# Contrast adjustment on one core: whole 32 KB rows, single first loads, and a first store that waits for the fifth load

## The chip, the cores and the metric

The kernel runs on one core of one Trainium2 chip. The metric is the time of one execution on the device in microseconds, as the median of several runs; lower is better. A profiled execution of the same program gives the trace. Its span runs from the first to the last instruction of the core, so it is a little shorter than the time that is measured around a run.

## The reference

```python
def setup_inputs():
    batch, c, h, w = 16, 3, 512, 512
    return {
        "x": np.random.rand(batch, c, h, w).astype(np.float32),
        "factor": np.float32(1.5),
    }

def reference(x, factor):
    mean = np.mean(x, axis=(2, 3), keepdims=True)
    return np.clip(mean + factor * (x - mean), 0, 1).astype(np.float32)
```

There are 48 images (16 x 3) of 512 x 512 numbers. Each number is moved away from its own image's mean by a factor of 1.5 and clipped to 0..1. The mean of an image must be known before any of its numbers can be written. Input and output are 50.33 MB each.

## The kernel before

**Tiles.** An image is 32 rows of `ROW` = 8192 numbers (32 KB a row). Four images make a tile of 128 rows, one to a partition, 4.19 MB; there are 12 tiles. On chip lies one tensor `ring` with `BUFS` = 6 slots (L64), and tile t lives in slot t modulo 6, is changed in place there and is stored from there. So load t + 6 can start only when store t has landed.

**Work on a tile.** `load` (L66 to L74) issues a DMA from the SP queue; with n = 2 it takes two tiles in one DMA, and either of them can be used only when the whole has landed. `add` (L86 to L90) is one activation on ScalarE (ACT) that copies the tile onto itself and adds up each row into a column of `sums`. `shift_by` (L92 to L96) multiplies the row sums by `blockw`, a block-diagonal matrix that holds (1 - factor) / pixels, on TensorE: each row gets its image's (1 - factor) x mean in `bias`, in PSUM. Each such product shows as two matmul records in the trace. `clip` (L76 to L84) is two instructions on VectorE (DVE): multiply by the factor and add the bias (L78), then cut to 0..1 (L82). `store` (L98 to L99) issues a DMA from the ACT queue.

**Queues and order.** The order is written out by hand (L101 to L126), and each engine takes its instructions in that order. ACT both computes the adds and issues the stores; a store that waits for its clip holds up the adds behind it, and an add that waits for its load holds up the stores behind it. SP only issues loads. Both queues' transfers run on the same 16 DMA engines.

**The start.** Tiles 0 and 1 are loaded by single DMAs, tiles 2 and 3 by one, tiles 4 and 5 by one. Tile 0 is summed in two halves at once, columns 0 to `SUM` = 4352 by a reduction on DVE (L108) and the rest by ACT. Its clip and store go in three pieces that end at `CUTS` = 1024, 3072 and 8192 columns, that is in rows of 4, 8 and 20 KB.

**The loop** over tiles 1 to 11 (L119 to L126) does, for tile t: the product, the clip, the add of tile t + 1, the store of t, and the load of t + 6. All its loads and stores are whole tiles.

Of the kernel before, what the change touches and what calls it, by code (L numbers as in the profile page):

```python
# [1 line left out]

# [4 lines left out]


P = 128  # L10
ROW = 8192
BUFS = 6
CUTS = (0, 1024, 3072, ROW)
SUM = 4352


@with_exitstack
def kernel(
    ctx: ExitStack,
    tc: tile.TileContext,  # L20
    x: bass.AP,
    factor: float,
    out: bass.AP,
):

    nc = tc.nc
    f32 = mybir.dt.float32
    Alu = mybir.AluOpType  # L30
    Act = mybir.ActivationFunctionType

    B, C, H, W = x.shape
    n_img, n_pix = B * C, H * W
    ppi = n_pix // ROW
    per_tile = P // ppi
    n_tiles = n_img // per_tile
    assert ppi * ROW == n_pix and per_tile * n_tiles == n_img

    factor = float(factor)  # L40
    wconst = (1.0 - factor) / float(n_pix)

    x_f = x.rearrange("b c h w -> (b c h w)")
    out_f = out.rearrange("b c h w -> (b c h w)")

    def dram(ap, t, c0=0, c1=ROW):
        return bass.AP(tensor=ap.tensor, offset=t * P * ROW + c0, ap=[[ROW, P], [1, c1 - c0]])

    consts = ctx.enter_context(tc.tile_pool(name="consts", bufs=1))
    xpool = ctx.enter_context(tc.tile_pool(name="xpool", bufs=1))  # L50
    small = ctx.enter_context(tc.tile_pool(name="small", bufs=1))
    psum = ctx.enter_context(tc.tile_pool(name="psum", bufs=1, space=bass.MemoryType.PSUM))


    sums = small.tile([P, 2 * n_tiles], f32, name="sums")
    bias = psum.tile([P, n_tiles], f32, name="bias")

    blockw = consts.tile([P, P], f32, name="blockw")
    nc.gpsimd.memset(blockw, 0.0)  # L59
    for a in range(0, P, ppi):  # L60
        nc.gpsimd.memset(blockw[a : a + ppi, a : a + ppi], wconst)  # L61


    ring = xpool.tile([P, BUFS, ROW], f32, name="ring")  # L64

    def load(t, c0=0, c1=ROW, n=1):  # L66

        b = t % BUFS
        src = bass.AP(
            tensor=x_f.tensor,  # L70
            offset=t * P * ROW + c0,
            ap=[[ROW, P], [P * ROW, n], [1, c1 - c0]],
        )
        nc.sync.dma_start(out=ring[:, b : b + n, c0:c1], in_=src)  # L74

    def clip(t, c0, c1):  # L76
        part = ring[:, t % BUFS, c0:c1]
        nc.vector.tensor_scalar(  # L78
            out=part, in0=part, scalar1=factor, scalar2=bias[:, t : t + 1],
            op0=Alu.mult, op1=Alu.add,  # L80
        )
        nc.vector.tensor_scalar(  # L82
            out=part, in0=part, scalar1=0.0, scalar2=1.0, op0=Alu.max, op1=Alu.min
        )  # L84

    def add(t, c0=0):  # L86
        part = ring[:, t % BUFS, c0:ROW]
        own = sums[:, 2 * t : 2 * t + 1]
        nc.scalar.activation(out=part, in_=part, func=Act.Copy, accum_out=own)  # L89
        return own  # L90

    def shift_by(t, *parts):  # L92
        for k, part in enumerate(parts):
            nc.tensor.matmul(  # L94
                bias[:, t : t + 1], blockw, part, start=k == 0, stop=k == len(parts) - 1
            )  # L96

    def store(t, c0, c1):  # L98
        nc.scalar.dma_start(out=dram(out_f, t, c0, c1), in_=ring[:, t % BUFS, c0:c1])  # L99

    with tc.manual_schedule():  # L101
        load(0)
        load(1)
        load(2, n=2)
        load(4, n=2)

        rest = sums[:, 1:2]
        nc.vector.tensor_reduce(  # L108
            out=rest, in_=ring[:, 0, 0:SUM], axis=mybir.AxisListType.X, op=Alu.add
        )  # L110
        shift_by(0, add(0, SUM), rest)
        for c0, c1 in zip(CUTS[:-2], CUTS[1:-1]):
            clip(0, c0, c1)
            store(0, c0, c1)
        clip(0, CUTS[-2], ROW)
        own = add(1)
        store(0, CUTS[-2], ROW)
        load(BUFS)
        for t in range(1, n_tiles):  # L119
            shift_by(t, own)  # L120
            clip(t, 0, ROW)
            if t + 1 < n_tiles:
                own = add(t + 1)
            store(t, 0, ROW)
            if t + BUFS < n_tiles:
                load(t + BUFS)  # L126


# [1 line left out]
_INS = ['x', 'factor']  # L130
_OUTS = [((16, 3, 512, 512), 'float32')]

_NUMBERS = {'factor': 1.5}


# [26 lines left out]
```

## Time and profile before

| what | value |
|---|---|
| median of 3 runs | 239.19 us (239.05 to 239.28) |
| the profiled execution's span | 237.8 us |
| activation of one whole tile (L89) | 7.03 us, and 0.19 to read the sum |
| the two clip instructions of one whole tile (L78, L82) | 4.49 and 4.43 us |
| issue of a store on ACT | 0.34 us |
| adds of tiles 8, 9, 10 and 11 start at | 137.75, 157.15, 176.56, 195.94 us |
| last store issued | 212.73 us |
| the same store, from issue to landing | 24.3 us |

The profile page lists each engine's busy time and the share of the span; below it stand the span in 40 slices, with the DMA engines' busy share in tenths (9 is 90% or more) and the rate of the bytes that they moved, and then the DMA queues with their packets, bytes, and the time of their packets as a share of 16 engines' span. A packet here is a row of a load or a store, or a small write that tells of a landing. The same three lines can be had for a stretch of the span; the share is then of that stretch, and it can be a little over 100% in sum because a packet is counted where it starts. Queue q1 holds the loads, q10 the stores.

What ACT mostly waits for is a load to land:

```profile
ACT ring L89 <- DMA ring<-in_x_dram: 119.4, 10, 19.6
```

(the engine, what it waited for, the time in all, the number of waits and the longest). SP's waits are all for stores, which free a slot of the ring:

```profile
SPq L74 <- DMA out_dram<-ring: 157.5, 8, 33.3
```

The DMA issues, with the size of each and the median time from issue to landing:

```profile
out_dram<-ring ACTq DMA_DIRECT2D x11, 4096.0 KB, 44.2
ring<-in_x_dram SPq DMA_DIRECT2D x8, 4096.0 KB, 33.3
ring<-in_x_dram SPq DMA_DIRECT2D x2, 8192.0 KB, 60.6
out_dram<-ring ACTq DMA_DIRECT2D x1, 2560.0 KB, 37.5
out_dram<-ring ACTq DMA_DIRECT2D x1, 1024.0 KB, 25.9
out_dram<-ring ACTq DMA_DIRECT2D x1, 512.0 KB, 16.1
```

### The profile page before, as it was taken

The page shows a single profiled execution, that of the slowest core. Times are in us where ns is not written, and L with a number is a line of the kernel's source. Part 1 is how long each engine was busy: PE and PEld are TensorE (multiplying, and loading weights), DVE is VectorE, ACT ScalarE, POOL GpSimd, SP SyncE. Part 2 cuts the span into 40 slices and gives each one's busy share as a digit, 9 for nine tenths or more (in the row PEclk, how much of TensorE's full clock was granted, in tenths as well). Part 3 has the DMA queues.
Part 4 walks back from the last instruction along what each step waited for, and adds up shares of the span by engine and source line. Part 5 has one row for each costly group of instructions (what it writes and reads, how often), then busy time and mean ns, then how long its engine had stood idle before and what let it go on. Part 6 is the DMA issues. An engine that isn't in the chain of part 4 may idle for free.

```text
span 237.8 us, 219 instructions
## 1 busy us (share of the span) xinstructions
PE 7.6 (3%) x26; PEld 6.5 (3%) x26; DVE 112.1 (47%) x29; ACT 82.9 (35%) x25; POOL 0.9 (0%) x9
## 2 busy tenths in 40 slices
PE   0010000000000000000000000000000000000000
PEld 0000000000000000000000000000000000000000
DVE  0078786009990039979407705902920950770000
ACT  2051900399000697380091083056038009100000
POOL 1000000000000000000000000000000000000000
DMA  7999999999999999999999999999999999999996
GB/s 265 441 441 442 401 471 429 391 413 430 457 441 435 413 408 430 435 435 441 441 441 441 441 435 435 402 419 430 435 441 441 441 441 441 441 430 413 413 430 259
DMA packets 3712, 100.66 MB, mean 423 GB/s; under 512 B 384, under 2 KB 384, under 8 KB 512
## 3 DMA queue, kind: packets, MB, share of 16 engines
q1 hardware_dynamic: 1696, 50.33, 49.6%
q10 hardware_dynamic: 2016, 50.33, 49.1%
HBM read 50.33 MB, written 50.33 MB: 423 GB/s over the span
## 4 chain that ended last, share of the span: by engine, by line
DMA 52%; another core or an unknown queue 15%; DVE 11%; issue 9%; PE 1%; ACT 1%; SPq 0%; ACTq 0%
DMA ring<-in_x_dram 33%; DMA out_dram<-ring 20%; DVE ring L78 6%; DVE ring L82 6%; PE bias L94 1%; ACT ring L89 1%; SPq L74 0%; ACTq L99 0%; ACTq L89 0%
## 5 line engine op out<-in xcount | busy, mean ns | idle before, releaser
L89 ACT ACTIVATE ring<-ring 128x8192 f32<-128x8192 f32 (+1 forms) x12 | 80.7, 6725 | 119.4 <-DMA ring<-in_x_dram 119.4
L78 DVE TENSOR_SCALAR ring<-ring,bias 128x8192 f32<-128x8192 f32 (+3 forms) x14 | 54.3, 3880 | 87.1 <-PE bias L94 87.1
L82 DVE TENSOR_SCALAR ring<-ring 128x8192 f32<-128x8192 f32 (+3 forms) x14 | 53.4, 3817 | 0.5
L94 PE MATMUL bias<-sums,blockw 128*128 128x1 f32 x26 | 7.6, 361 | 196.1 <-ACT ring L89 195.6
L94 PEld LDWEIGHTS bias<-sums,blockw 128*128 128x128 f32 x26 | 6.5, 311 | 197.1 <-ACT ring L89 179.9
L108 DVE TENSOR_REDUCE sums<-ring 128x1 f32<-128x4352 f32 x1 | 4.7, 4686 | 13.0 <-DMA ring<-in_x_dram 13.0
L89 ACT ACTIVATION_READ_ACCUMULATOR ring<-ring 128x1 f32 x12 | 2.2, 186 | 0.0
L89 ACT ACT_TABLE_LOAD x1 | 1.3, 1283 | 0.7 <-PEq L143 0.7
L61 POOL MEMSET blockw<- 32x32 f32 x4 | 0.5, 116 | 0.2
L59 POOL MEMSET blockw<- 128x128 f32 x1 | 0.2, 205 | 0.3 <-POOLq L143 0.3
L143 POOL MEMSET const-bfloat16-1.0<- 128x1 bf16 x1 | 0.1, 111 | 0.0
L143 POOL MEMSET const-uint8-127<- 128x1 uint8 x1 | 0.1, 111 | 0.0
L143 POOL MEMSET const-float32-1.0<- 128x1 f32 x1 | 0.1, 108 | 0.0
L143 POOL MEMSET const-float32-0.0<- 128x1 f32 x1 | 0.1, 103 | 0.2 <-issue 0.2
## 6 DMA issues: line engine op xcount, KB each, us to landing
out_dram<-ring ACTq DMA_DIRECT2D x11, 4096.0 KB, 44.2
ring<-in_x_dram SPq DMA_DIRECT2D x8, 4096.0 KB, 33.3
ring<-in_x_dram SPq DMA_DIRECT2D x2, 8192.0 KB, 60.6
out_dram<-ring ACTq DMA_DIRECT2D x1, 2560.0 KB, 37.5
out_dram<-ring ACTq DMA_DIRECT2D x1, 1024.0 KB, 25.9
out_dram<-ring ACTq DMA_DIRECT2D x1, 512.0 KB, 16.1
```

The costliest lines, as they stand in the source:

```text
L59: nc.gpsimd.memset(blockw, 0.0)
L61: nc.gpsimd.memset(blockw[a : a + ppi, a : a + ppi], wconst)
L78: nc.vector.tensor_scalar(out=part, in0=part, scalar1=factor, scalar2=bias[:, t : t + 1], op0=Alu.mult, op1=Alu.add,)
L82: nc.vector.tensor_scalar(out=part, in0=part, scalar1=0.0, scalar2=1.0, op0=Alu.max, op1=Alu.min)
L89: nc.scalar.activation(out=part, in_=part, func=Act.Copy, accum_out=own)
L94: nc.tensor.matmul(bias[:, t : t + 1], blockw, part, start=k == 0, stop=k == len(parts) - 1)
L108: nc.vector.tensor_reduce(out=rest, in_=ring[:, 0, 0:SUM], axis=mybir.AxisListType.X, op=Alu.add)
L143: nc = _bacc.Bacc("TRN2", target_bir_lowering=False, num_devices=1)
```

## The change

All loads and stores become whole single tiles: `load` and `store` lose their column ranges, and `load` its n. The first six loads are issued one by one, so there are 12 loads and 12 stores, where there were 10 and 14. `CUTS`, `SUM` and the reduction on DVE go; every tile is summed by ACT alone and clipped whole.

The order of the start is new. Tiles 0 to 3 are summed and clipped as they come, and nothing is stored. Tile 4 (`gate` = 4, the fifth load) is summed by two activations, the first over only `FIRST` = 512 columns; between the two stand store(0) on ACT and load(6) on SP. As ACT works in order and the short activation waits for load 4, store(0) goes out only after that load. Stores 1 to 3 and loads 7 to 9 follow after tile 4's product and clip are in their queues. From tile 5 on, the loop does add(t), product, clip, store(t), load(t + 6): the add of tile t + 1 now stands behind store(t) on ACT, where it stood before it.

```diff
-CUTS = (0, 1024, 3072, ROW)
-SUM = 4352
+FIRST = 512
...
-    def load(t, c0=0, c1=ROW, n=1):
+    def load(t):
+        nc.sync.dma_start(out=ring[:, t % BUFS, :], in_=dram(x_f, t))
...
-        nc.sync.dma_start(out=ring[:, b : b + n, c0:c1], in_=src)
+    def store(t):
+        nc.scalar.dma_start(out=dram(out_f, t), in_=ring[:, t % BUFS, :])
...
-    def add(t, c0=0):
-        part = ring[:, t % BUFS, c0:ROW]
-        own = sums[:, 2 * t : 2 * t + 1]
+    def add(t, c0=0, c1=ROW):
+        part = ring[:, t % BUFS, c0:c1]
+        k = 2 * t + (c0 > 0)
+        own = sums[:, k : k + 1]
         nc.scalar.activation(out=part, in_=part, func=Act.Copy, accum_out=own)
         return own
...
     with tc.manual_schedule():
-        load(0)
-        load(1)
-        load(2, n=2)
-        load(4, n=2)
+        for t in range(BUFS):
+            load(t)
 
-        rest = sums[:, 1:2]
-        nc.vector.tensor_reduce(
-            out=rest, in_=ring[:, 0, 0:SUM], axis=mybir.AxisListType.X, op=Alu.add
-        )
-        shift_by(0, add(0, SUM), rest)
-        for c0, c1 in zip(CUTS[:-2], CUTS[1:-1]):
-            clip(0, c0, c1)
-            store(0, c0, c1)
-        clip(0, CUTS[-2], ROW)
-        own = add(1)
-        store(0, CUTS[-2], ROW)
+
+        gate = BUFS - 2
+        for t in range(gate):
+            shift_by(t, add(t))
+            clip(t)
+        first = add(gate, 0, FIRST)
+        store(0)
         load(BUFS)
-        for t in range(1, n_tiles):
-            shift_by(t, own)
-            clip(t, 0, ROW)
-            if t + 1 < n_tiles:
-                own = add(t + 1)
-            store(t, 0, ROW)
+        shift_by(gate, first, add(gate, FIRST))
+        clip(gate)
+        for t in range(1, gate):
+            store(t)
+            load(t + BUFS)
+        for t in range(gate, n_tiles):
+            if t > gate:
+                shift_by(t, add(t))
+                clip(t)
+            store(t)
             if t + BUFS < n_tiles:
                 load(t + BUFS)
```

More of the change, by code (lines that the diff above doesn't have):

```diff
@@ L37 @@
     n_tiles = n_img // per_tile
-    assert ppi * ROW == n_pix and per_tile * n_tiles == n_img
+    assert ppi * ROW == n_pix and per_tile * n_tiles == n_img and n_tiles > BUFS
     factor = float(factor)
@@ L44, with dram @@
     out_f = out.rearrange("b c h w -> (b c h w)")
-    def dram(ap, t, c0=0, c1=ROW):
-        return bass.AP(tensor=ap.tensor, offset=t * P * ROW + c0, ap=[[ROW, P], [1, c1 - c0]])
+    def dram(ap, t):
+        return bass.AP(tensor=ap.tensor, offset=t * P * ROW, ap=[[ROW, P], [1, ROW]])
     consts = ctx.enter_context(tc.tile_pool(name="consts", bufs=1))
@@ L64, with shift_by, clip @@
     ring = xpool.tile([P, BUFS, ROW], f32, name="ring")
-    def load(t, c0=0, c1=ROW, n=1):
[L68 to L72, printed above, removed]
-        )
-        nc.sync.dma_start(out=ring[:, b : b + n, c0:c1], in_=src)
-    def clip(t, c0, c1):
-        part = ring[:, t % BUFS, c0:c1]
+    def load(t):
[3 more added lines that the diff above has]
+    def add(t, c0=0, c1=ROW):
+        part = ring[:, t % BUFS, c0:c1]
+        k = 2 * t + (c0 > 0)
+        own = sums[:, k : k + 1]
+        nc.scalar.activation(out=part, in_=part, func=Act.Copy, accum_out=own)
+        return own
+    def shift_by(t, *parts):
+        for k, part in enumerate(parts):
+            nc.tensor.matmul(
+                bias[:, t : t + 1], blockw, part, start=k == 0, stop=k == len(parts) - 1
+            )
+    def clip(t):
+        part = ring[:, t % BUFS, :]
         nc.vector.tensor_scalar(
@@ L84, in clip @@
         )
-    def add(t, c0=0):
-        part = ring[:, t % BUFS, c0:ROW]
-        own = sums[:, 2 * t : 2 * t + 1]
[L89 to L99, printed above, removed]
-    with tc.manual_schedule():
-        load(0)
-        load(1)
-        load(2, n=2)
-        load(4, n=2)
-        rest = sums[:, 1:2]
-        nc.vector.tensor_reduce(
-            out=rest, in_=ring[:, 0, 0:SUM], axis=mybir.AxisListType.X, op=Alu.add
-        )
-        shift_by(0, add(0, SUM), rest)
-        for c0, c1 in zip(CUTS[:-2], CUTS[1:-1]):
-            clip(0, c0, c1)
-            store(0, c0, c1)
-        clip(0, CUTS[-2], ROW)
-        own = add(1)
-        store(0, CUTS[-2], ROW)
-        load(BUFS)
-        for t in range(1, n_tiles):
-            shift_by(t, own)
-            clip(t, 0, ROW)
-            if t + 1 < n_tiles:
-                own = add(t + 1)
-            store(t, 0, ROW)
+    with tc.manual_schedule():
+        for t in range(BUFS):
[6 more added lines that the diff above has]
+        store(0)
+        load(BUFS)
+        shift_by(gate, first, add(gate, FIRST))
[8 more added lines that the diff above has]
+            store(t)
             if t + BUFS < n_tiles:
```

## The prediction

> **What bounds the kernel now.** I read the page's busy shares and DMA rows first:
>
> ```profile
> span 237.8 us, 219 instructions
> ...
> PE 7.6 (3%) x26; PEld 6.5 (3%) x26; DVE 112.1 (47%) x29; ACT 82.9 (35%) x25; POOL 0.9 (0%) x9
> ...
> DMA  7999999999999999999999999999999999999996
> GB/s 265 441 441 442 401 471 429 391 413 430 457 441 435 413 408 430 435 435 441 441 441 441 441 435 435 402 419 430 435 441 441 441 441 441 441 430 413 413 430 259
> DMA packets 3712, 100.66 MB, mean 423 GB/s; under 512 B 384, under 2 KB 384, under 8 KB 512
> ...
> q1 hardware_dynamic: 1696, 50.33, 49.6%
> q10 hardware_dynamic: 2016, 50.33, 49.1%
> ```
>
> No compute engine is busy for half the span, while the DMA engines are full in all slices but the first and the last. The two queues (q1 the loads, from SP; q10 the stores, from ACT) hold 98.7% of 237.8 us, that is 234.7 us. So 3.1 us lie outside the transfers, at head and tail, and the rest can only shrink if the same 100.66 MB take less engine time per byte, or if a hole that doesn't exist now is not opened.
>
> Next I asked the DMA view for single stretches. First 35 to 55 us, where the stores of tile 0's second and third piece run beside loads:
>
> ```profile
> DMA packets 415, 8.31 MB, mean 416 GB/s; under 512 B 47, under 2 KB 47, under 8 KB 47
> ## 3 DMA queue, kind: packets, MB, share of 16 engines
> q1 hardware_dynamic: 207, 6.26, 76.0%
> q10 hardware_dynamic: 208, 2.05, 24.1%
> ```
>
> and 100 to 195 us, where whole 32 KB rows go both ways:
>
> ```profile
> DMA packets 1421, 41.35 MB, mean 435 GB/s; under 512 B 159, under 2 KB 159, under 8 KB 159
> ## 3 DMA queue, kind: packets, MB, share of 16 engines
> q10 hardware_dynamic: 719, 20.94, 51.0%
> q1 hardware_dynamic: 702, 20.41, 49.8%
> ```
>
> Both are full, so engine time per MB is the price. Whole rows: 100.8% of 95 us = 95.76 us for 41.35 MB, 2.316 us per MB. Pieces: 100.1% of 20 us = 20.02 us for 8.31 MB, 2.409. That the first is the floor is borne out by the timeline: in the steady part the activations of L89 start at 118.33, 137.75, 157.15, 176.56 and 195.94 us, 19.40 apart, a load and a store each time: 9.70 us a tile (4.19 MB x 2.316 = 9.71).
>
> **What the change is worth, part by part.**
>
> *Store rows.* Tile 0's store loses its 4, 8 and 20 KB pieces. The excess of 35 to 55 us over the floor is 20.02 - 8.31 x 2.316 = 0.77 us. For 20 to 35 us the same view gives 89.1% + 8.5% of 15 us for 6.29 MB, 14.64 - 14.57 = 0.07 us. 55 to 100 us gives 100.4% of 45 us for 19.51 MB, 2.316 again: no excess. Together 0.84 us. The trace doesn't say whether small rows or the first meeting of loads and stores cause it, so the bounds are 0 (it comes back when mixing begins) and 0.84. I take 0.8, since the stage after the change mixes whole rows only, as 55 to 195 us did.
>
> *Two activations in place of a reduction at the start.* The 4352-element reduction (4.69 us) and the 3840-element activation (3.40 us) go; tile 0 is summed by one of 7.03 us. It ends some 2.5 us later, before nothing that is needed until 52 us: cost 0.
>
> *Single loads.* SP issues six instead of four, from 0.74 us on and one every 0.45 us (the chain of waits has issues at 0.74, 1.17 and 1.64), so the last at about 3.0 us, when one tile of 9.7 us is under way: 0. Bytes and rows are the same. Tiles 2 to 5 become available one by one instead of in pairs.
>
> *The gated first store.* From the add that waited for load 0, which starts at
>
> ```profile
> 13.01 3.40 ACT L89 ACTIVATE ring<-ring 128x3840 f32<-128x3840 f32 x1 [10.98 <-DMA ring<-in_x_dram]
> ```
>
> and with loads alone on the engines, loads 1 to 4 land at 22.7, 32.4, 42.1 and 51.8 us. An add of load t takes 7.03 + 0.19, the matmul 0.6, the clip 4.49 + 4.43: 17 us with the gaps. Tiles 0 to 3 are clipped at 29.9, 39.6, 49.3 and 59.0. ACT is free from 49.3 and waits for load 4. The 512-element add is not in the trace; from the two forms of L89, (7.03 - 3.40) / 4352 elements = 0.83 ns each and 0.2 us fixed, so 0.63 us, between 0.4 (the pure rate) and 3.4 (the shorter form seen); I take 0.63, as both forms lie on that line. Store(0) is then issued at about 52.7. Queued behind it on ACT: the 7680-element add (6.6 us, to 59.5), then stores 1 to 3 at 0.34 us each, to 60.6 (tile 3 is clipped at 59.0), then store 4, which waits for its clip until 69.5, then the add of tile 5. Nobody waits for these yet but the DMA queue. Load 5 keeps the engines busy meanwhile: at 52.7 it has 8.8 us left, and with equal shares (10.03 and 9.48 MB in 55 to 100 us) it lands near 70 and store 0 at 13.0 + 6 x 9.70 = 71.2. Cost of the gate: 0, covered by load 5; were stores 1 to 3 not yet queued at 71.2, every us of delay would be lost.
>
> *Loads 6 to 11* wait on SP for stores 0 to 5. Load 6 is issued at 71.3, against 65.67 now; 29 us of stores cover the 1 to 5 us until its first bytes (both worked out under the rivals). Stores then land about every 19.4 us from store 1 (near 90), each releasing a load while its predecessor still runs. Loads land near 91, 111, 130, 149, 169, 188.
>
> *The new loop order.* add(t + 1) now stands behind store(t) on ACT, which waits for clip(t). So a tile is a serial chain of 7.22 + 0.6 + 8.92 + 0.34 and gaps of 0.2: 17.3 us against 19.4 us a tile. It is hidden with 2.1 us a tile to spare, and by more than one finished tile in the store queue. Store 11 is issued near 188 + 17.3 = 205, when 31 us of transfers, 3.2 tiles, are left until 236; without store 11 that is 2.2 tiles in the queue ahead of it, 21 us: the tail stays full. If the chain were over 19.4 us, the surplus would first eat this backlog.
>
> **Sum.** 237.8 - 0.8 = 237.0 us of span. A second count agrees: 13.0 for load 0, 23 more tiles at 9.70 give the last landing at 236.1; now it is at 237.0 (issued at 212.73, landing 24.3 us later). That is 0.9 less. Medians stand 239.19 - 237.8 = 1.4 us above the span, so **238.4 us**. Known ends of the sum alone: 239.2 (excess comes back) and 237.9 (0.9, and 0.4 of the 0.58 us excess of the first 20 us, 18.78 - 7.86 x 2.316, in case it is not all start-up).
>
> **Rivals.**
>
> *Row size isn't the cause: no change.* Then mixing itself, wherever it begins, costs 0.8 us, and it begins here too. For it: in 20 to 35 us, with 4 KB rows, the smallest, the excess is only 0.07 us. Against it: from 55 us mixing goes on and costs nothing. Time: 239.2, or 238.8 with half of it.
> The Trainium skill, "DMA: Bandwidth & Descriptors", section "Why small descriptors are slow (HBM only)", speaks for this rival: it states a fixed overhead of about 3 cycles per packet beside one beat per 32 bytes. By it, as an estimate, 4 KB rows cost 2.0% more than 32 KB rows, 8 KB 0.9%, 20 KB 0.2%, on an eighth, a quarter and five eighths of one tile, 0.06 us in all, which would make 239.1 us. The 0.77 us row stands against its size, unless something else than row size makes that excess.
>
> *The engines run dry once, near 71 us: slower.* The store queue then holds only store 0 if ACT hasn't passed the second add and stores 1 to 3 before 71.2, and load 6 cannot start before store 0 has landed. Place: ACT, between store(0) and store(1). It decides if ACT is held there more than 10.6 us beyond 60.6, for instance because a store waits for an earlier transfer's landing that its data doesn't need. For it: ACT's in-order queue does hold stores back today (store 1, clipped at 39.5, goes out at 45.65 behind the add that waits for a paired load); against it: nothing in the code ties store 1 to store 0. Price: from 71.2 to the first byte. At least 1 us: the first load is issued at 0.74 and the DMA view of 0 to 5 us has its first bytes at 1.75. At most 5 us: tile 0's first piece took 16.1 us to land, of which its eight rows an engine, each behind a load row, explain 8 x (1.21 + 0.16) = 11.0 (9.70 / 8; 8.5% of 15 us x 16 / 128). On 238.4 that makes 239.4 to 243.4, middle 241.4.
>
> *The chain of 17.3 us becomes the bound.* Needed: stores 4 to 11 ready one chain apart, from 69.5, 190.6 at the latest for tile 11, while the stores' own transfers last to 236. Little speaks for it; time 238.4 unless it exceeds some 22 us a tile, (226 - 69.5) / 7.
>
> **Chances.** Forecast (0.8 us gained): 0.61, with its own range 237.8 to 238.8. No change, from row size not being the cause: 0.17. Engines dry once, or the chain: 0.22. A measurement of this kernel can tell about 0.2%, 0.48 us, from no change. The forecast's upper edge and half of the no-change case's partial gain cancel, so faster 0.61, same 0.17, slower 0.22. The range 237.8 to 239.9 holds the forecast, no change, and the shortest dry spells.
>
> **What would show it.** The 35 to 55 us stretch should have loads alone until about 53 to 56 us at 2.316 us per MB; store 0 should be issued within 1.5 us of load 4's landing; q1 + q10 should hold about 233.9 us in all; SP's first wait for a store should end near 71; no slice of the DMA row but the first and last should fall below 9. I am wrong if a slice near 66 to 76 us dips, if the chain of waits goes through ACT's stores, or if packet time stays at 234.7 us.

## The result and the profile after

The changed kernel takes 239.86 us (median of 6 runs, 239.22 to 240.49), the kernel before 239.12 us (6 runs, 238.68 to 239.28): a ratio of 1.0033, 95% interval 1.0019 to 1.0047. It is slower by 0.33%, and its runs lie 1.3 us apart, where those of the kernel before lie 0.6 us apart. In a later session, experiment e1 below, the ratio was 1.0016 (1.0001 to 1.003).

The profiled execution is the quickest of the six, 239.22 us; its span of 237.4 us is even 0.4 us shorter than the one shown of before. From its page, the rate of the DMA engines in 40 slices and the two queues:

```profile
span 237.4 us, 203 instructions
...
DMA  7999999999999999999999999999999999999996
GB/s 265 442 442 442 436 420 442 431 420 392 431 436 420 414 442 442 442 442 431 442 420 431 431 420 431 442 442 442 442 431 425 431 436 425 414 442 442 442 442 265
DMA packets 3456, 100.66 MB, mean 424 GB/s; under 512 B 384, under 2 KB 384, under 8 KB 384
...
q1 hardware_dynamic: 1728, 50.33, 49.8%
q10 hardware_dynamic: 1728, 50.33, 49.1%
```

98.9% of 237.4 us is 234.8 us of transfers, against 234.7 before. The small rows are gone (3456 packets for 3712), and no time went with them: of the prediction's signs of being wrong, the last one came. The lowest of the middle slices, 392 GB/s, is the tenth, from 53 to 59 us. The DMA view of 45 to 65 us, where store 0 joins the loads:

```profile
DMA packets 268, 8.26 MB, mean 413 GB/s; under 512 B 16, under 2 KB 16, under 8 KB 16
## 3 DMA queue, kind: packets, MB, share of 16 engines
q1 hardware_dynamic: 204, 6.16, 75.2%
q10 hardware_dynamic: 64, 2.10, 24.3%
```

99.5% of 20 us for 8.26 MB, at 2.316 us per MB: 19.90 - 19.13 = 0.77 us too much (the excess, from here on), the same amount that the kernel before paid between 35 and 55 us. The trace also records each row's start and duration. It doesn't name the row's engine, but a row begins where one before it ends, to within 0.01 us for nearly all, so the rows can be put together into 16 engines, of 192 rows of 32 KB each. Every engine's last load row before its first store row (56.5 us and on) took 1.6 to 2.05 us instead of 1.21.

ACT in the timeline at the gate (start, duration, engine, line; ACTq is ACT's queue issuing a DMA; x2 stands for two instructions in one line):

```profile
52.00 0.63 ACT L71 ACTIVATE ring<-ring 128x512 f32<-128x512 f32 x1 [2.59 <-DMA ring<-in_x_dram]
52.01 0.86 ACTq L65 DMA_DIRECT2D out_dram<-ring  x2
52.53 0.19 ACT L71 ACTIVATION_READ_ACCUMULATOR ring<-ring 128x1 f32 x1
52.63 6.59 ACT L71 ACTIVATE ring<-ring 128x7680 f32<-128x7680 f32 x1
52.91 6.50 ACTq L65 DMA_DIRECT2D out_dram<-ring  x2
```

The gate works: the first store goes out 0.01 us after the activation that waited for load 4 starts, and not when that activation ends. Stores 0 and 1 are one line here (x2), store 2 follows at 52.91 while the long activation runs, store 3 at 59.1 when tile 3 is clipped. After that no slice shows the engines idle, load 6 is issued at 72.14 us, and the last add starts at 193.07 us. So the quick execution holds nothing that would explain 239.86; the traces of longer ones, in the experiments, do.

### The profile page after: what moved, and what is told of

It reads as the page before. It is cut to its first block, busy times and chain, and to the rows that moved or that the text cites. A ratio compares the mean times of both kernels' runs of the same rounds, so it can differ in the third digit from the quotient of the medians.

```text
span 237.4 us, 203 instructions
## 1 busy us (share of the span) xinstructions
PE 7.6 (3%) x26; PEld 6.5 (3%) x26; DVE 107.0 (45%) x24; ACT 86.9 (37%) x27; POOL 0.9 (0%) x9
## 2 busy tenths in 40 slices
DMA packets 3456, 100.66 MB, mean 424 GB/s; under 512 B 384, under 2 KB 384, under 8 KB 384
## 4 chain that ended last, share of the span: by engine, by line
DMA 47%; another core or an unknown queue 32%; DVE 4%; ACT 3%; SPq 1%; issue 0%; PE 0%
DMA ring<-in_x_dram 32%; DMA out_dram<-ring 15%; ACT ring L71 3%; DVE ring L82 2%; DVE ring L86 2%; SPq L62 1%; PE bias L76 0%
## 5 line engine op out<-in xcount | busy, mean ns | idle before, releaser
L71 ACT ACTIVATE ring<-ring 128x8192 f32<-128x8192 f32 (+2 forms) x13 | 84.5, 6503 | 112.5 <-DMA ring<-in_x_dram 102.4
L82 DVE TENSOR_SCALAR ring<-ring,bias 128x8192 f32<-128x8192 f32 x12 | 53.9, 4492 | 102.4 <-PE bias L76 102.4
L86 DVE TENSOR_SCALAR ring<-ring 128x8192 f32<-128x8192 f32 x12 | 53.1, 4427 | 0.4
```

The lines of the kernel that those rows point to most:

```text
L82: nc.vector.tensor_scalar(out=part, in0=part, scalar1=factor, scalar2=bias[:, t : t + 1], op0=Alu.mult, op1=Alu.add,)
L86: nc.vector.tensor_scalar(out=part, in0=part, scalar1=0.0, scalar2=1.0, op0=Alu.max, op1=Alu.min)
```

## The experiments

For the excess where stores join, the same count as above is made each time from the DMA view of the 15 to 35 us around it. The theories' letters (O, R, E and so on) are explained in the expectations.

**e1 and e2: both kernels again.** No edit.

> The changed kernel once more, for a second trace and more times. Theory O (onset): wherever stores first join a full load queue, some 30 load rows take up to 2 us instead of 1.21, 0.8 us of engine time in all, whatever the row size; so the 0.8 us are back between 52 and 57 us, and what varies from run to run is this onset: a slower run than 237.4 us of span shows more than 0.8 us of slowed rows there, and the runs spread over 1 us again, median 239.6 to 240.1. Rival R (row size): small rows cost the 0.8 us before, the onset costs nothing by itself, and the extra time of slow runs lies elsewhere, at the head or in the tail.

> The kernel before once more, to see how much its own runs and its slowed rows differ between two traces. Both theories: 239.1 us, runs within 0.6 us of each other, excess over 2.316 us per MB near 0.8 us between 20 and 55 us.

The changed kernel: 239.47 us (11 runs, 238.9 to 240.87), ratio 1.0016 (1.0001 to 1.003). The kernel before: 238.99 us (11 runs, 238.9 to 239.29), and 239.02 over 27 further runs beside these (238.79 to 239.44). The excess is 0.62 us in the traced run of e1 (238.9 us) and, over 20 to 55 us, 0.72 in that of e2. So the two kernels' best runs are equal within 0.1 us, and the changed kernel has a long upper end.

**e3: whole first store in the kernel before.**

```diff
-        for c0, c1 in zip(CUTS[:-2], CUTS[1:-1]):
-            clip(0, c0, c1)
-            store(0, c0, c1)
-        clip(0, CUTS[-2], ROW)
+        clip(0, 0, ROW)
         own = add(1)
-        store(0, CUTS[-2], ROW)
+        store(0, 0, ROW)
```

> The kernel before with tile 0 clipped whole and stored by one DMA of 32 KB rows at about 28 us; paired loads, early stores and loop order stay. Theory O: the excess of 0.8 us is paid at one place when this store joins, time 239.1 within 0.4 us. Rival R: no small rows, no excess, 238.3 us.

239.24 us (11 runs, 239.01 to 240.52), ratio 1.0017 (1.0005 to 1.003). In 20 to 40 us:

```profile
DMA packets 270, 8.32 MB, mean 416 GB/s; under 512 B 16, under 2 KB 16, under 8 KB 16
## 3 DMA queue, kind: packets, MB, share of 16 engines
q1 hardware_dynamic: 208, 6.29, 77.4%
q10 hardware_dynamic: 62, 2.03, 23.5%
```

20.18 us for 8.32 MB: an excess of 0.91 us with no small row in the kernel. The row-size theory (R) falls: a kernel without small rows pays as much. The single rows show where it is paid. In e3 it is in the load rows from 29 to 31 us, ahead of the first 32 KB store row at 32.3 us; where the stores resume at 56.5 us after a pause, no load row is slow, so it is paid once. In the kernel before, in both of its traces, the 4 KB rows that first join the loads at 23 us slow hardly any load row. The slow ones stand ahead of the first 8 KB row (0.1 to 0.3 us too long, near 35 us) and about the first 20 KB rows (0.1 to 0.6 us, 47 to 52 us), and in one of the traces at 41 us. So the cost belongs to the stores' coming on beside the loads: at once with whole rows (0.91 us here), in steps while the rows grow (0.84 and 0.72 us).

**e4: the gate at tile 1.** `gate = 1` in place of `BUFS - 2`.

> The changed kernel with the gate at tile 1 instead of tile 4: the first store is issued when the second load has landed and tile 0 is clipped, near 30 us; whole rows, single loads and the new loop order stay. Theory O with the late gate as what makes the onset cost vary (three stores issued within 1 us): 239.1 us and a spread below 0.6 us, since one store joins alone. If single loads or the loop order are what costs: 239.8 us as with the late gate. Rival R: 238.4 us or the same as with the late gate.

243.63 us (5 runs), ratio 1.0189 (1.0164 to 1.0214). Neither theory had that: an early gate alone makes the new form 4 us slower. In this trace load and store tiles land within 2.3 to 3.2 us of each other from 51 to 194 us, and the DMA view of the last microseconds shows the engines out of step: rows begin in groups a fraction of a row time apart, the last of them at 239.6 us. The page's chain of waits runs through DVE for 41% of the span and ACT for 24%, which looks like the prediction's rival of the 17.3 us chain. But no slice but the first and the last shows idle engines, and the two queues hold 98.2% of 241.9 us, 237.5 us, against 234.8 in the changed kernel: the rows took longer.

**e5: store 0 in pieces, at the gate.** `store(0)` becomes three stores, columns 0 to 1024, to 3072, to 8192.

> The changed kernel, but store 0 goes out at the gate in three DMAs with rows of 4, 8 and 20 KB, as in the kernel before; all else stays. Theory O2 (after the first runs): the onset of stores in a full load queue costs about 0.8 us in any kernel, and with whole 32 KB rows it costs more in some runs (up to 2 us more), while small first rows spread it out and keep it near 0.8. Then the spread of the changed kernel falls from 2 us to under 0.7 us and the median from 239.5-239.9 to 238.8-239.1. Rival L: the spread comes from the late gate, the single loads or the loop order; then it stays at 1 us or more, median 239.5 to 239.9.

239.79 us (6 runs, 239.57 to 240.23), ratio 1.0031 (1.002 to 1.0042). The spread is smaller, as O2 had it, in no more than six runs, but the median stays, so O2 falls: small first rows don't take the cost away. The excess in 55 to 70 us is 0.72; again the slow load rows (58 to 61 us) stand ahead of the first 8 KB row at 62.4 us, and hardly any ahead of the first 4 KB row at 55.8 us.

**e6: FIRST = 6144.**

> The changed kernel with FIRST = 6144 instead of 512: the short add of tile 4 takes 5.3 us instead of 0.6, so store 0 is issued at about 57.3 instead of 52.5 us, and its first rows come when load 5 is all but done (it would end alone at 61.6; the first store row came 4.5 us after its issue). Theory O2: with hardly a load row left to be slowed, the excess of 0.8 us before 60 us goes, span 236.5 to 237.0, times 238.3 to 238.8 and a small spread, unless the engines idle between the last load row and the first store row. Rival L: 239.5 to 239.9 and the same spread.

239.08 us (12 runs, 238.63 to 240.15), ratio 1.0007 (0.9995 to 1.002). The premise was wrong: store 0 went out at 51.87 us, while the 6144-column activation ahead of it ran until 57.19. So this edit hardly moves a transfer, and the run tells nothing of the theories. It is a third sample of the changed kernel's transfers, and shows how far medians of such a spread can differ: the three ratios are 1.0033, 1.0016 and 1.0007.

**e7 and e15: single first loads in the kernel before.**

```diff
-        load(2, n=2)
-        load(4, n=2)
+        for t in range(2, BUFS):
+            load(t)
```

> The kernel before with six single first loads in place of two single and two paired ones; early stores in pieces and the loop order stay. Theory O2: 239.0 us, spread below 0.7 us, since the first stores have small rows. Rival L, if it is the single loads: 239.5 us or a spread over 1 us.

> The kernel before with six single first loads, once more, for a trace of one of its slow executions (250 to 254 us in four of six). If falling behind is what makes it slow: the engines' last transfers end many us apart, the mean well before the last. If the rows themselves are slow throughout: all end late together, with an excess over 2.316 us per MB of some 10 us.

e7 gave 242.40, 242.49, 250.31, 251.66, 252.29 and 253.88 us: this part alone, beside early stores, costs 1.4% in the two quick runs and 4.7 to 6.2% in the four long ones, at a granted clock of 1.0 in all six. The trace of e7 itself is of the run of 242.49 us: from 236.2 us on rows begin only one or two at a time, the last at 238.2 us. e15 caught one of the long ones, 251.4 us. Its page:

```profile
DMA  7999899999999999999999999999999999998910
GB/s 268 473 436 427 385 476 432 379 433 431 467 420 415 420 410 410 441 431 431 410 446 425 420 415 436 425 410 431 425 420 415 446 446 431 425 425 383 425 53 37
```

The span is 249.6 us, a slice 6.2 us. In the last two slices 53 and 37 GB/s move, where all 16 engines together move 433: two engines (2/16 of 433 is 54) work alone for some 10 us, and the other 14 are done near 237.5 us. That is the first alternative of the expectation in its plainest form; the packet time, 94.9% of 249.6 us or 236.9 us, is only 2 us longer than before. The 14 take over no row of the two. **A DMA is split over 16 engines in fixed shares, and the kernel ends with the engine that is furthest behind.**

**e8: the loop order of before**, add(t + 1) ahead of store(t), from the add of tile 5 on.

> The changed kernel with the loop order of before (the add of tile t + 1 stands ahead of store t on ACT), from tile 5 on. Theory O2: no effect, median 239.5 to 239.9 and a spread over 1 us as the changed kernel. Rival L, if it is the loop order: 239.0 us and a spread below 0.7 us.

239.97 us (10 runs, 238.99 to 240.65), ratio 1.0032 (1.0018 to 1.0046): no effect, as O2 said. Its traced run is a long one (239.8 us, span 238.0). Store rows that began between 52 and 58 us, in e1 and then in e8:

```profile
q10 hardware_dynamic: 16, 0.52, 20.2%
```

```profile
q10 hardware_dynamic: 15, 0.49, 19.0%
```

In e1 all 16 engines have begun a store row, in e8 one has not. In the single rows that engine's load row at 54.87 us took 2.88 us, where the others' took 1.64 to 1.91: it lost one row time (1.21 us) more at the meeting, and it ends 1.0 us after the next to last engine.

**e9: the gate at tile 5.** `gate = BUFS - 1`.

> The changed kernel with the gate one tile later: store 0 waits for the sixth load, so it joins an empty load queue. Theory E (what the runs so far suggest): wherever stores join running loads, each of the 16 engines spends 0.5 to 0.8 us more on the load row before its first store row, which gives back the forecast gain, and in part of the runs one engine loses about a row (1.2 us) more there and ends last alone; that is the spread. With no load row left to slow, the excess after the first 5 us falls under 0.2 us and the runs lie within 0.6 us of each other, while the engines idle 1.0 to 1.5 us near 61.6 us (a first load's bytes come 1.0 us after its issue): 239.3 to 239.7 us. Rival L2 (the spread comes from the later part, the waits of loads for stores or the tail): the runs spread over 1 us as before, median 240.5 or more.

242.21 us (5 runs, 241.79 to 242.91), ratio 1.0138 (1.0119 to 1.0157). A miss: with nothing to overlap, the start of the stores costs more. Its page has two dips, the 11th slice (60 to 66 us, loads run out, stores begin) and the 14th (78 to 84 us, near where loads come back):

```profile
DMA  7999999999699899999999999999999999999996
GB/s 262 437 437 437 437 437 437 437 437 437 262 437 410 382 431 426 431 437 437 426 426 426 431 437 410 431 437 437 437 437 437 437 437 437 437 437 437 437 437 262
```

The overlap that costs 0.8 us at the gate of tile 4 is the cheaper way. The single rows show the parts. Each engine stands idle for 1.4 to 2.0 us near 61 us, where E had 1.0 to 1.5, and the first store rows are at full speed (1.21 us). But where the loads come back, at 77.7 us, each engine has a store row of 1.7 to 2.4 us just ahead: the excess that E put at under 0.2 us is paid there, when loads first join running stores. The spread of 1.1 us doesn't fit E either.

**e10 and e13: the gate at tiles 2 and 3.**

> The changed kernel with the gate at tile 2: store 0 is issued when load 2 has landed, at 32.4 us, tile 0 being clipped at 30. Theory P for the 243.6 us of the gate at tile 1: there a load's and a store's tile ended within 2.5 us of each other all along (70.9 and 73.2, 90.8 and 93.2 us ...), and the rows after such a boundary are slowed and the engines drift apart. With the gate at 2 the ends should be 8 to 9 us apart, as with the gate at 4, and the time as there: 239.3 to 239.9 us. Rival: an early gate is bad in itself, because few stores are queued with the new loop order: 241 us or more.

> The changed kernel with the gate at tile 3: store 0 goes out when load 3 has landed, near 42.1 us, and load 6 is issued before load 5 has landed, so the load queue never runs empty. Theory H2 (an engine falls behind where a queue that ran empty starts again, as loads do near 72 us with the gate at 4): 238.9 to 239.3 us and a spread under 0.8 us, as with the gate at 2. Theory H1 (it falls behind because three stores are issued within 1 us at the first meeting; here it is two): between the two, 239.2 to 239.6, and a spread over 1 us.

Gate at 2: 239.10 us (12 runs, 238.78 to 239.78), ratio 1.0001 (0.9991 to 1.0012), level with the kernel before. An early gate isn't bad in itself, as theory P had it, and the ends of load and store tiles are at least 7.2 us apart in this trace. Gate at 3: 239.47 us (11 runs, 239.06 to 239.86), ratio 1.0015 (1.0006 to 1.0024). Here the load queue never runs empty (load 6 is issued at 67.44 us, and load rows go on without a gap), and still 7 of 11 runs are over 239.4, so H2 falls. The excess at the meeting is 0.81 and 0.92 us.

**e11 and e12: the changed kernel, two more traces.**

> The changed kernel unchanged, one more trace, to tie a run's span to its last engine. Theory E: the mean end of the 16 engines' transfers is 235.5 to 236.0 us whatever the span, and a span over 237.5 us goes with one or two engines that end later than the rest, with one load row near 54 us that took over 2.3 us. Rival L2: in a slow run all engines end later.

> The changed kernel unchanged, a further trace for the same question: the mean end is 235.5 to 236.0 us, and the span follows the last engine alone (Theory E), or all engines end later in a slow run (Rival L2).

239.38 and 240.13 us. The DMA view of 234 to 238 us (each slice 0.1 us; a packet is counted where it starts, one 32 KB row in a slice is 328 GB/s), first of e1 (238.9 us), then of e12 (240.13 us):

```profile
DMA  0099990700000000000000000000000000000000
GB/s 0 0 655 1311 983 1966 0 328 0 0 0 0 0 0 0 0 0 0 0 0 0 0 0 0 0 0 0 0 0 0 0 0 0 0 0 0 0 0 0 0
```

```profile
DMA  0099979977000000000700000000000000000000
GB/s 0 0 655 983 1311 328 655 655 328 328 0 0 0 0 0 0 0 0 0 328 0 0 0 0 0 0 0 0 0 0 0 0 0 0 0 0 0 0 0 0
```

In e1 sixteen rows begin between 234.2 and 234.7, each engine's last. In e12 sixteen begin between 234.2 and 234.9 and a single one at 235.9: one engine is a row behind. The spans differ by 1.2 us (237.1 and 238.4), and so do the last rows' starts (234.7 and 235.9). Theory E holds in this, and the mean end of the 16 engines is 235.8 us in e12 and 236.0 in e11, as it had it. Its place for the loss doesn't always hold: in e12 no load row near 54 us took over 2.3 us, and the late engine shows only in the landings from 88 us on. Its rows lost 1.05 us at the meeting, where the others lost 0.5 to 0.8, and then 0.2 to 0.5 us each at 56.9, 87.4, 92.7 and 126.8 us.

**e14: stores 1 to 3 later.** `own = add(gate + 1)` stands ahead of the loop over stores 1 to 3, so store 0 meets the loads alone.

> The changed kernel (gate at 4) with the add of tile 5 ahead of stores 1 to 3 on ACT, so that store 0 alone meets the loads at 52 us and stores 1 to 3 go out near 68 us, when load 5 has landed and store 0 has some 3 us left. Theory H1: 238.9 to 239.3 us and a spread under 0.8 us. Theory H2: 239.5 to 239.9 us and a spread over 1 us as the changed kernel, since loads still stop at 68 and start again after 72 us.

239.78 us (12 runs, 239.14 to 241.95), ratio 1.0037 (1.0019 to 1.0054); in its trace three engines end a row late. H1 falls. H2's numbers fit here, but e13 has ruled it out.

In the ten traces of the changed kernel's form with the gate at 2, 3 or 4, the span goes with the start of the last row:

| traced run | most engines' last row starts | the very last row starts | span |
|---|---|---|---|
| e6 | 234.1 to 234.4 | 234.4 | 236.8 |
| e1 | 234.2 to 234.5 | 234.7 | 237.1 |
| e10 | 234.4 to 234.8 | 234.8 | 237.2 |
| the result's | 234.4 to 234.8 | 235.0 | 237.4 |
| e11 | 234.5 to 235.0 | 235.2 | 237.6 |
| e8 | 234.2 to 234.6 | 235.6 | 238.0 |
| e13 | 234.3 to 234.8 | 235.7 | 238.1 |
| e5 | 234.3 to 235.1 | 235.6 | 238.2 |
| e14 | 234.3 to 234.7 | 235.8 | 238.2 |
| e12 | 234.2 to 234.9 | 235.9 | 238.4 |

The difference of the last two columns is 2.4 to 2.6 us in all.

## Why the prediction was wrong

**The bound and the stream of work: right.** DMA transfers bound both kernels. Loads alone (20 to 45 us of the changed kernel), both together (100 to 190 us of it) and stores alone (196 to 236 us of the kernel before) move at the same price, 2.316, 2.316 and 2.315 us per MB. No dry spell came near 71 us, nor did the chain of 17.3 us bind.

**The gate: right in its effect, wrong in one detail.** Stores 1 and 2 were to be queued behind the 7680-column add until 59.5 us. ACT's queue issued them at 52.5 and 52.9 us, the second while it ran. No run shows that this cost or saved anything: in e14 they go out from 68.7 us on, and its median of 239.78 us lies between the changed kernel's 239.47 and 239.86.

**Store rows: the step that failed.** The sum took 0.8 us of gain out of bounds 0 and 0.84. Zero was right. The excess is 0.77 us in the changed kernel and lies between 0.4 (e6) and 1.0 us (e11) in the traces in which stores join running loads, with small rows or without. The choice of the value was argued from 55 to 195 us, where mixing was already under way; the cost is of the stores' coming on, and that the change only moves and puts in one place. It was a rival, with a chance of 0.17. The row that spoke for it, hardly any excess beside the 4 KB rows, did show that the smallest rows are not what costs. The rule of the Trainium skill that stood beside it ("DMA: Bandwidth & Descriptors", "Why small descriptors are slow (HBM only)") put small rows at 0.06 us, as an estimate; e3, which has none and is not faster, agrees with it that they are cheap, though its runs can't resolve 0.06 us.

**The span it started from: of a long run.** In all runs on record that have both, the time is 1.73 to 1.83 us above the span, but for one with 2.06. The sum put 1.4 us between them, as it took the span of one run and the median of others. By 1.8 us a run with a span of 237.8 us takes some 239.6 us, more than any of the three timed ones, and the sum would have come to 238.8. What made it long is one engine, in the DMA view of its 234 to 238 us:

```profile
DMA  0099999000000070000000000000000000000000
GB/s 0 0 655 655 1966 1311 655 0 0 0 0 0 0 0 328 0 0 0 0 0 0 0 0 0 0 0 0 0 0 0 0 0 0 0 0 0 0 0 0 0
```

One row starts at 235.4 us, after the others' 234.2 to 234.6. So the second count, which found 0.9 us between the last landing at 237.0 and the 236.1 of an even stream, found mostly this engine and not the store rows; that it agreed with 0.8 was luck. In e2, the same kernel, the last tile lands at 236.5 us.

**What no step had: the slowest of 16 engines.** Engine time per MB, counted over all 16, gives the mean end, and that hardly differs between the two kernels: 235.8 us in both traces of the kernel before, 235.7 to 236.0 in the four of the changed one. The end is the latest engine's, 0.9 and 0.4 us after the mean before the change, 0.4, 0.3, 0.5 and 1.4 us after it. In the long runs one engine, in e14 three, is a row (1.2 us) behind. So the missing term is 0 to 1.2 us, more in single runs, and by the medians more often not 0 after the change: that is the 0.16 to 0.33%.

**The order of the two parts mattered.** Single loads alone cost 3 to 15 us (e7); with the gate at tile 1 4.6 us are left (e4), and from tile 2 on nothing of that kind (e10). The prediction put single loads at 0 by bytes and issue times; beside the gate that holds, by itself it doesn't.

**Open.** Why an engine falls behind more often with the gate at 3 or 4 than at 2 or in the kernel before was not settled: neither three stores at once (e14 is without them) nor loads that run out and start again (e13 is without that) are needed for it, and neither row size nor the loop order changed it (e5, e8). Why two engines drift further at each tile with single loads and early stores (e7, e15), and why a paired load prevents it, wasn't found either. One thing sets the three slow kernels apart in the landings: between 85 and 192 us a load tile and a store tile land within 0.2 us of each other in e15, 2.3 to 3.1 in e4 and 2.4 to 3.9 in e7, and at least 5.2 us apart in all other traces. And only in these three does the time from the first to the last engine's share of a landing keep growing in that stretch, by 2 to 6 us, against 0.7 at most elsewhere. That fits theory P, but no run set this distance alone, so it is an observation and not a cause shown. No version tried beats the kernel before; the gate at 2 equals it.

## What to carry to other kernels

When DMA engines are full from start to end, what is left is how two queues begin to share them and whether all engines end together, so read the last microseconds of the DMA view row by row before pricing bytes. An excess in a stage may belong to the beginning of an overlap and not to the form of its transfers; then moving the beginning keeps it. And for a change of some tenths of a per cent one trace is not enough: a long run of the kernel before stood beside the quickest of the changed one, and that looked like a gain.

## What the runs showed that was not expected

- 32 KB store rows that join running loads make the load row ahead of them slower on each engine, 1.6 to 2.0 us instead of 1.21, once; with rows of 4, 8 and 20 KB the 4 KB ones cost next to nothing, and the loss comes with the longer ones. Starting stores on engines that have just run out of loads cost more: 1.4 to 2.0 us idle, and the slow rows all the same when the loads come back (e9, 3 us in all).
- Engines that fell out of step didn't catch up in the long runs: in e15 two of 16 end some 10 us after the rest, which take over none of their rows.
- ACT's queue issues a DMA while an activation that stands ahead of it in program order still runs (store 0 at 51.87 us, the activation from 51.86 to 57.19, in e6).
